# RWKV layer of a two-layer decoder trunk: causal masks, Gram products and the first T products tied to other matmuls

## The chip, the core and the metric

The kernel runs on one core of one Trainium2 chip. The core has five engines that run their own instruction queues in order and wait for each other through semaphores: TensorE (PE, with its weight loads as PEld), VectorE (DVE), ScalarE (ACT), GpSimd (POOL) and SyncE (SP), beside 16 DMA engines. The metric is the time on the device in microseconds (us) of one execution; lower is better. Three runs of the kernel before are there, and one more execution was taken by the hardware profiler.

## The reference

An input of 512 tokens by 2048 channels in float32 passes two residual layers, first a gated differential attention, then a gated RWKV-7 time mixing. The change lies in the second. Cut to what matters:

```python
def rwkv7_mixer(h, ...):
    p = h @ w_in                          # r, k, v, gate: 2048 columns each; decay and rate: 96 each
    p = p + (token_shift(p) - p) * mu
    r, k, v, g, dw, da = split(p)
    decay = exp(-exp(-softplus(-(w0 + tanh(dw) @ decay_up)) - 0.5))
    a = sigmoid(a0 + da @ iclr_up)
    kk = heads(k * k_k); kk = kk / norm(kk)
    k = k * (1 + (a - 1) * k_a)
    y = wkv7_scan(r, decay, k, v, -kk, kk * a)      # 32 heads of 64 channels
    y = group_norm(y) + sum(r * k * r_k) * v
    return (y * silu(g)) @ w_out

def step(S, r, w, k, v, a, b):            # one token of one head, S is 64 x 64
    sa = S @ a
    S = S * w + outer(sa, b) + outer(v, k)
    return S, S @ r
```

## The kernel before

**Tiling.** The second layer works on 16 pairs of heads, `j` = 0 to 15, of 128 channels each. For each pair there are four projections (`k`, `r`, `v` and, three pairs late, the gate). One is 48 matmuls of 128x128 weights by 512 tokens on TensorE: 16 slices of the 2048 inputs, each as three products of high and low parts (`mm3`, L129). The weights come in raw by DMA, are cast to `wh` on ScalarE (L115), and VectorE makes the rest `wl` (L116). "The 27th receptance matmul" is a place in such a run of 48: hooks in the list `behind` are called when their number of matmuls has been issued.

**The scan.** The 512 tokens are cut into 8 chunks of 64, and a chunk's recurrence is made of matrix products. For a pair this takes, in order: `stage1` and `stage2` build `AR` (the scaled kk and r; L1122 finishes it with the receptances) and `BK`; `gram` multiplies `BK` by `AR` for all chunks (`gp`, L1137), and ScalarE copies the parts into `LP` (L1145) and the whole into `G` (L1150). `mask_gram` clears what is not causal in `G`, with four `affine_select` on POOL, two of 64x512 (L1182) and two of 64x1024 elements (L1184). `t_solve` inverts a triangular 32x32 matrix for each chunk and half on VectorE: it transposes `LP` to `LT` (L1216), scales by `n` (the norms of the keys, which come over a DMA issued on POOL), then makes 31 steps of a product (L1230) and a sum (L1233) on `Tm`, then transposes to `T` (L1238, the tile `T1`) and to `W` (L1243); POOL copies `W` into `TT` (four copies, L1249) and fills a new `Tm` from `unit` (L1220). `t_first` and `t_second` are two groups of small products on TensorE (`px`, L1264 from `T`, and L1279 from `W`) with ScalarE copies, which complete `TT`.

Then `scan_pair` goes through the 8 chunks. Each has three products on TensorE one after the other: `sm` from `VS` and `G` (L1356), from `rhs` and `TT` (L1369), from `VS` and `BKT` (L1378). Between them ScalarE copies (L1359, L1371), and the state is renewed by VectorE (`VS`, L1385 for the first chunk, L1382 later), which needs `Sg` from POOL (L1364 copies `SA`, L1367). At the end stand the outputs `Y` (L1402, L1406) and their normalisation on VectorE and ScalarE (L1417 to L1433).

**What sets the order.** The program is written for a list scheduler, which puts each engine's instructions in one fixed order. All pairs are staggered: while the projections of pair `j` run, the scan of pair `j-1` is woven in as a generator whose steps come every few matmuls (`Chain`, `tick`), and the solve of pair `j` is another generator (`Solve`): a `yield n` in `t_solve` lets n matmuls pass. A hook's work is placed behind its matmul by `issue_after` (on TensorE) or by `behind` (masks and solve), which gives the scheduler an order without a semaphore; when the chip runs it, the engine's own queue and true data dependences decide. `LAG` is 3; the hooks are 12, 15 or 18 in the value projection for `gram`, and in the receptance projection of the next pair 6 for the masks, 12 and 33 for the two `px` groups and 39 or 45 for the norms.

Of the kernel before, what the change touches and what calls it, by code (L numbers as in the profile page):

```python
# [942 lines left out]
@urgent  # L943
def shift_mix(g, ps, rows, mu, omu, tag, bufs=2):

    nc, w = g.nc, g.work
    o_ = w.tile([P, T], F32, name="mix" + tag, tag=tag, bufs=bufs)
    nc.scalar.activation(o_[:rows, :], ps[:rows, :], AF.Copy, scale=omu)
    nc.vector.scalar_tensor_tensor(o_[:rows, 1:], ps[:rows, 0 : T - 1], mu, o_[:rows, 1:], ALU.mult, ALU.add)
    return o_  # L950
# [77 lines left out]
LAG = 3  # L1028
# [6 lines left out]
def mus(g, i, j):  # L1035
    n = i * 16 + j
    return g.mu[:, n : n + 1], g.omu[:, n : n + 1]
# [121 lines left out]
def norms(g, j, p, m):  # L1159

    nc, w = g.nc, g.work
    while g.later:
        g.later.pop(0)()
    ps = g.ps.tile([P, 512], F32, name="pt", tag="pb", bufs=2)
    with g.tc.issue_after(m.ins):
        sum_channels(g, ps[:2, :], g.ones[:, 0 : P : C], p.k2)
    ss = w.tile([2, T], F32, name="ssl", tag="thg", bufs=1)
    nc.scalar.copy(ss[:].rearrange("h (b c t) -> h c b t", b=2, c=NC_), ps[:2, :].rearrange("h (c b t) -> h c b t", c=NC_, b=2))
    nd = g.nd[j % 2]
    for half in range(2):  # L1170
        x = ss[:, half * NC_ * HALF : (half + 1) * NC_ * HALF]
        nc.gpsimd.dma_start(out=nd[:, half].rearrange("h r c t -> h r (c t)"),
                            in_=x[:, None].to_broadcast([2, NG, NC_ * HALF]))
    p.n2 = g.small.tile([P, HALF], F32, name="n2", tag="n2", bufs=1)
    nc.gpsimd.dma_start(out=p.n2[:], in_=nd.rearrange("h b r c t -> (h b r c) t"))


def mask_gram(g, p, h, m=None):

    nc = g.nc  # L1180
    for r_ in [slice(h * C, h * C + C)]:
        a = nc.gpsimd.affine_select(out=p.G[r_, :, 0, 1 - h, :], in_=p.G[r_, :, 0, 1 - h, :], compare_op=ALU.is_ge,  # L1182
                                fill=0.0, base=-1, pattern=[[0, NC_], [1, C]], channel_multiplier=-1)
        b = nc.gpsimd.affine_select(out=p.G[r_, :, 1], in_=p.G[r_, :, 1], compare_op=ALU.is_ge, fill=0.0, base=0,  # L1184
                                pattern=[[0, NC_], [0, 2], [1, C]], channel_multiplier=-1)
        behind(g, a, m)
        behind(g, b, m)


def turn_keys(g, p, c0):  # L1190

    nc = g.nc
    if not c0:
        p.BKT = g.work.tile([P, NC_, P], F32, name="BKT", tag="BKT", bufs=2)
    ps = g.ps.tile([P, 512], F32, name="pt", tag="pb", bufs=2)
    for i in range(4):
        nc.tensor.transpose(ps[:, i * P : (i + 1) * P], p.BK[:, c0 + i].rearrange("p s t -> p (s t)"), g.ident[:])
    nc.scalar.copy(p.BKT[:, c0 : c0 + 4], ps[:].rearrange("p (c k) -> p c k", c=4))


def behind(g, ins, m=None):

    m = m or g.at
    if m:
        g.tc.add_manual_dep(ins.ins, m.ins.name, mybir.DependencyInfo(mybir.DependencyClass.NoSync,
                            mybir.DependencyReason.DATA), reason="pace")


def t_solve(g, j, p):


    nc, w = g.nc, g.work
    NQ = HALF // NG
    yield 6
    LT = w.tile([P, HALF, HALF], F32, name="LT", tag="LT", bufs=1)
    lt = nc.vector.transpose(LT[:].rearrange("p (r c) t -> p t r c", r=NG),  # L1216
                        p.LP[:].rearrange("p c t -> p t c")[:, :, None, :].to_broadcast([P, HALF, NG, NC_]))
    Tm = w.tile([P, NQ, HALF], F32, name="Tm", tag="Tm", bufs=1)
    tmp = w.tile([P, NQ * HALF], F32, name="tmpl", tag="tmpl", bufs=1)
    nc.gpsimd.tensor_copy(Tm[:], g.unit[:])  # L1220
    n2 = p.n2
    behind(g, lt)
    with g.tc.issue_after(lt.ins):
        nc.vector.tensor_scalar(n2[:], n2[:], 1e-24, None, ALU.max)
        nc.vector.reciprocal(n2[:], n2[:])
    yield 9 if j >= LAG else 3
    for i in range(HALF - 1):
        n, s = HALF - 1 - i, i // NG + 1
        tt = tmp[:, : n * s].rearrange("p (a b) -> p a b", a=s)
        st = nc.vector.scalar_tensor_tensor(tt, LT[:, i : i + 1, i + 1 :].to_broadcast([P, s, n]), n2[:, i : i + 1],  # L1230
                                       Tm[:, 0:s, i : i + 1].to_broadcast([P, s, n]), ALU.mult, ALU.mult)
        behind(g, st)
        nc.vector.tensor_add(Tm[:, 0:s, i + 1 :], Tm[:, 0:s, i + 1 :], tt)  # L1233
        yield 3 + i % 2
    nc.vector.tensor_mul(Tm[:], Tm[:], n2[:, None, :].to_broadcast([P, NQ, HALF]))
    p.T1 = w.tile([P, NC_, HALF], F32, name="T1", tag="T1", bufs=1)
    yield 9
    tt = nc.vector.transpose(p.T1[:].rearrange("p c (q r) -> p q r c", r=NG),  # L1238
                        Tm[:].rearrange("p q (r c) -> p q r c", r=NG))
    p.W = w.tile([P, NC_, HALF], F32, name="W", tag="Tm", bufs=1)  # L1240
    behind(g, tt)
    yield 4
    tt = nc.vector.transpose(p.W[:], p.T1[:])  # L1243
    behind(g, tt)
    for h in range(2):
        for half in range(2):
            o = half * HALF
            q = slice(h * C + o, h * C + o + HALF)
            nc.gpsimd.tensor_copy(g.TT[j % 2][q, :, h, o : o + HALF], p.W[q])  # L1249
# [72 lines left out]
def gated(g, j, p, gt, last=False):  # L1322
    g.nc.vector.tensor_mul(gt[:], gt[:], p.y[:])
    if last:
        return
    g.nc.scalar.dma_start(out=g.yd2[j * P : (j + 1) * P, :], in_=gt[:])
# [118 lines left out]
def layer1(g, aps):  # L1445
    nc, tc = g.nc, g.tc
    with ExitStack() as cx:
# [5 lines left out]
        pairs = []  # L1453

        def proj(i, j, **k):
            return unit_chan(g, [(win, i * D + j * P, P)], P, **k)[0]
# [10 lines left out]
        def receptances(j):  # L1467
            def piece(f, i, p):
                def follow(m):
                    with tc.high_priority(offset=SCAN), tc.issue_after(m.ins):  # L1470
                        f(g, i, p)
                return follow

            behind = [(45 if j == 1 else 39, lambda m: norms(g, j, pairs[j], m))]
            if j:
                behind += [(6, lambda m: [mask_gram(g, pairs[j - 1], h, m) for h in range(2)]),
                           (12, piece(t_first, j - 1, pairs[j - 1])),
                           (33, piece(t_second, j - 1, pairs[j - 1]))]
            return shift_mix(g, proj(0, j, behind=behind), P, *mus(g, 0, j), "r", 1)

        begin(0)
        r = receptances(0)
        for j in range(D // P):
            p = pairs[j]
            if j:
                others = [(1, lambda p=p: turn_keys(g, p, 0)), (2, lambda p=p: turn_keys(g, p, 4)),
                          (4, lambda p=p: turn_values(g, p))]
                if j > 1:
                    others.append((5, lambda i=j - 2: finish_y(g, i, pairs[i])))
                full = LAG <= j < D // P - 1  # L1490
                gaps = (7, 8) if full else (5, 6) if j == 2 else (4, 5) if j == 1 else (6, 7)
                chain(g, j - 1, pairs[j - 1], 3 if j > 1 else 22, *gaps, others)
            stage2(g, j, r, p)

            def behind(m, j=j, p=p):
                if j > 1:
                    pairs[j - 2].chain.finish(g)
                with tc.issue_after(m.ins):
                    gram(g, j, p)
                p.solve = Solve(g, t_solve(g, j, p))  # L1500
            hooks = [(12 if 0 < j < LAG else 15 if j else 18, behind)]
            if j + 1 == D // P:
                hooks.append((39, lambda m, p=p: [mask_gram(g, p, h, m) for h in range(2)]))
            stage_v(g, j, p, proj(2, j, behind=hooks))
            turns = ()
            if j == 0:
                turns = ((9, lambda m: turn_keys(g, p, 0)), (15, lambda m: turn_keys(g, p, 4)),
                         (27, lambda m: turn_values(g, p)))
            if j + 1 < D // P:
                begin(j + 1, turns)  # L1510
            if j >= LAG:
                gated(g, j - LAG, pairs[j - LAG], gate(g, j - LAG, proj(3, j - LAG)))
            if j + 1 < D // P:
                r = receptances(j + 1)
# [121 lines left out]
```

## Time and profile before

| | us |
|---|---|
| median of three runs | 2165.76 |
| lowest and highest of them | 2164.96, 2167.0 |
| the profiled execution | 2167.01 |
| its span, first to last instruction | 2165.1 |
| second layer's pairs 4 to 14: one pair's period (`gp` to `gp`) | 60.9 |
| busy in the 60 us from 1480: PE, DVE, ACT, POOL | 58.82, 52.61, 37.05, 17.44 |

The granted TensorE clock is 0.999 of full speed. The second layer's pairs run from about 1014 to 1970 us of the span. Engines are named as in the section on the chip; L12 is line 12 of the kernel. In the timeline a row gives the start in us, the length in us, engine, line, operation and tiles, and in brackets the idle time of its engine before it and what ended that. Rows that follow each other are pipelined, so their lengths overlap a little; a step's cost is read from start to start. Profiled matmul ends are modelled.

### The profile page before, as it was taken

How to read it: one execution, taken by the hardware profiler on the slowest of the kernel's cores; microseconds unless marked ns; L12 is line 12 of the kernel's file. 1: busy time of each engine (PE TensorE's matmuls, PEld its weight loads, DVE VectorE, ACT ScalarE, POOL GpSimd, SP SyncE). 2: the span in 40 equal slices, each digit the busy share in tenths (PEclk: the TensorE clock that was granted, in tenths of full speed). 3: DMA queues.
4: the chain of work that ended last, by engine and by line, in shares of the span. 5: the costliest groups of instructions: out<-in, count | busy, mean ns of one | idle time of the engine just before them, and what ended most of it. 6: DMA issues, size and time to landing. Idle time of an engine off the chain costs nothing.

```text
span 2165.1 us, 34929 instructions
## 1 busy us (share of the span) xinstructions
PE 2129.7 (98%) x12260; PEld 1752.7 (81%) x12260; DVE 1557.4 (72%) x4137; ACT 1126.3 (52%) x2587; POOL 337.4 (16%) x614
## 2 busy tenths in 40 slices
PE   9999999999999999999999999999999999999999
PEld 7888888888888877888777888878887888877887
DVE  5665647465656667467889888888888888887645
ACT  6443444343444455345566665666666665665333
POOL 0000000000000000011132332233333332232001
PEclk9999999999999999999999999999999999999999
DMA  6223232322223365662322222232222223345565
GB/s 196 90 88 98 79 102 85 96 94 87 92 88 98 98 204 177 189 138 84 88 60 67 76 67 79 77 85 76 76 76 77 76 67 79 82 129 173 188 169 120
DMA packets 258623, 225.76 MB, mean 104 GB/s; under 512 B 12336, under 2 KB 220480, under 8 KB 258448
## 3 DMA queue, kind: packets, MB, share of 16 engines
q1 hardware_dynamic: 239504, 188.03, 29.4%
q0 software_dynamic: 10080, 19.50, 4.5%
q10 hardware_dynamic: 8864, 16.01, 2.0%
q8 instruction: 96, 1.57, 0.3%
q14 instruction: 79, 0.65, 0.1%
HBM read 207.50 MB, written 15.99 MB: 103 GB/s over the span
## 4 chain that ended last, share of the span: by engine, by line
PE 82%; DVE 11%; ACT 3%; issue 3%; DMA 1%; ACTq 0%; DVEq 0%
PE pp L129 63%; PE pt L129 5%; DVE wl L116 2%; PE gp L1137 1%; DVE tmpl L1230 1%; PE o L129 1%; PE sc L129 1%; PE sm L1356 1%; PE lora L129 1%; DVE Tm L1233 1%; PE sm L1378 1%; ACT wh L115 1%; DMA yr<-yd 1%; PE Y L1402 1%; PE sm L1369 1%
## 5 line engine op out<-in xcount | busy, mean ns | idle before, releaser
L116 DVE TENSOR_TENSOR wl<-wraw,wh 128x512 fp32r<-128x512 f32 (+1 forms) x636 | 449.6, 709 | 345.5 <-ACT wh L115 336.6
L115 ACT CAST wh<-wraw 128x512 fp32r<-128x512 f32 (+1 forms) x636 | 392.8, 619 | 499.6 <-PE pp L129 391.9
L129 PE MATMUL pp<-wh,hH 128*128 128x512 f32 x1268 | 500.2, 394 | 0.7 <-DVE prmin_rw_mu_dram L234 0.6
L129 PE MATMUL pp<-wh,hL 128*128 128x512 f32 x1268 | 497.5, 393 | 0.1
L129 PE MATMUL pp<-wl,hH 128*128 128x512 f32 x1268 | 497.2, 392 | 0.0
L129 PE MATMUL pp<-hH,wh 128*128 128x512 f32 x1024 | 417.5, 408 | 0.0
L129 PE MATMUL pp<-hL,wh 128*128 128x512 f32 x1024 | 413.2, 404 | 0.0
L129 PE MATMUL pp<-hH,wl 128*128 128x512 f32 x1024 | 412.7, 403 | 0.0
L129 PEld LDWEIGHTS pp<-wh,hH 128*128 128x128 f32 x1268 | 238.3, 188 | 49.9 <-issue 1.7
L129 PEld LDWEIGHTS pp<-wh,hL 128*128 128x128 f32 x1268 | 238.2, 188 | 49.2 <-DVE hL L908 0.5
L129 PEld LDWEIGHTS pp<-wl,hH 128*128 128x128 f32 x1268 | 238.3, 188 | 46.9
L129 PEld LDWEIGHTS pp<-hH,wh 128*128 128x128 f32 x1024 | 193.0, 189 | 37.3 <-issue 1.8
L129 PEld LDWEIGHTS pp<-hH,wl 128*128 128x128 f32 x1024 | 193.2, 189 | 33.4
L129 PEld LDWEIGHTS pp<-hL,wh 128*128 128x128 f32 x1024 | 193.2, 189 | 32.0
L1230 DVE SCALAR_TENSOR_TENSOR tmpl<-LT,n,Tm 128x60 f32<-128x60 f32 (+24 forms) x496 | 148.4, 299 | 12.1
L1364 POOL COPY SA<-VS 64x64 f32<-64x64 f32 x224 | 72.4, 323 | 513.2 <-DVE VS L1382 441.6
L500 POOL DMA_DIRECT2D frow<-yd x12 | 8.9, 742 | 801.8 <-DVE rs_t L67 675.9
L1233 DVE TENSOR_TENSOR Tm<-Tm,tmpl 128x60 f32<-128x60 f32 (+24 forms) x496 | 114.5, 231 | 13.1
L1359 ACT COPY rhs<-sm 64x64 f32<-64x64 f32 x256 | 52.6, 205 | 63.2 <-PE sm L1356 60.4
L1371 ACT COPY VS<-sm 64x64 f32<-64x64 f32 x256 | 52.8, 206 | 58.2 <-PE sm L1369 51.7
L1382 DVE SCALAR_TENSOR_TENSOR VS<-sm,gam,Sg 64x64 f32<-64x64 f32 x192 | 54.0, 281 | 30.6 <-PE sm L1378 26.3
L1356 PEld LDWEIGHTS sm<-VS,G 128*128 128x128 f32 x256 | 46.5, 188 | 26.1 <-PE pp L129 13.1
(339 smaller groups left out, 3268.0 us busy)
## 6 DMA issues: line engine op xcount, KB each, us to landing
wraw<-in_rw_w_in_dram SPq DMA_DIRECT2D x128, 512.0 KB, 4.0
wraw<-in_da_w_in_dram SPq DMA_DIRECT2D x254, 256.0 KB, 3.0
wraw<-in_da_w_out_dram SPq DMA_DIRECT2D x26, 512.0 KB, 4.3
wraw<-in_rw_w_out_dram SPq DMA_DIRECT2D x26, 512.0 KB, 4.3
yr<-yd SPq DMA_DIRECT2D x28, 256.0 KB, 3.9
frow<-yd POOLq DMA_DIRECT2D x12, 512.0 KB, 7.1
xq<-in_x_dram SPq DMA_DIRECT2D x16, 256.0 KB, 5.4
xd<-xq ACTq DMA_DIRECT2D x16, 256.0 KB, 4.1
```

Of the source, the lines that this page charges most:

```text
L115: nc.scalar.copy(hi[:], raw[:, k : k + n])
L116: nc.vector.tensor_sub(lo[:], raw[:, k : k + n], hi[:].bitcast(F32))
L129: m = nc.tensor.matmul(out, a, b, start=s, stop=e, skip_group_check=skip)
L1137: m = nc.tensor.matmul(gp[h][:, i * P : (i + 1) * P], BK[r_, c0 + i, :, :], p.AR[r_, c0 + i, :, :], start=True, stop=True)
L1230: st = nc.vector.scalar_tensor_tensor(tt, LT[:, i : i + 1, i + 1 :].to_broadcast([P, s, n]), n2[:, i : i + 1], Tm[:, 0:s, i : i + 1].to_br ...
L1233: nc.vector.tensor_add(Tm[:, 0:s, i + 1 :], Tm[:, 0:s, i + 1 :], tt)
L1356: nc.tensor.matmul(sm[:, 0:P], both(p.G[:, c, 0]), both(VS[:, c]), start=True, stop=True)
L1359: rc = nc.scalar.copy(rhs[r_, :], sm[r_, h * C : h * C + C])
L1364: nc.gpsimd.tensor_copy(p.SA[r_, c - 1, :], VS[r_, c, h, :])
L1369: nc.tensor.matmul(sm[:, P : P + C], both(g.TT[j % 2][:, c]), rhs[:], start=True, stop=True)
L1371: vc = nc.scalar.copy(VS[r_, c, h, :], sm[r_, P : P + C])
L1382: g.state = nc.vector.scalar_tensor_tensor(VS[r_, c + 1, h, :], s_, p.gam[r_, c : c + 1], Sg[r_, :], ALU.mult, ALU.add)
```

## The change

The masks of pair `j-1` are tied to the 27th receptance matmul in place of the 6th. The Gram products of pairs 3 to 15 come behind the 18th value matmul in place of the 15th. The solve's first pause is 3 matmuls in place of 6, and its second 10 or 6 in place of 9 or 3, so that counted from the value projection's start the transposition stands where it stood in pairs 3 to 15, and the first step one matmul later. For pair 0 alone the two `px` groups are tied to the 18th and 39th matmul in place of the 12th and 33rd.

```diff
 def t_solve(g, j, p):
-    yield 6
+    yield 3
     LT = w.tile([P, HALF, HALF], F32, name="LT", tag="LT", bufs=1)
...
-    yield 9 if j >= LAG else 3
+    yield 10 if j >= LAG else 6
     for i in range(HALF - 1):
...
             if j:
-                behind += [(6, lambda m: [mask_gram(g, pairs[j - 1], h, m) for h in range(2)]),
-                           (12, piece(t_first, j - 1, pairs[j - 1])),
-                           (33, piece(t_second, j - 1, pairs[j - 1]))]
+                behind += [(27, lambda m: [mask_gram(g, pairs[j - 1], h, m) for h in range(2)]),
+                           (12 if j > 1 else 18, piece(t_first, j - 1, pairs[j - 1])),
+                           (33 if j > 1 else 39, piece(t_second, j - 1, pairs[j - 1]))]
...
-            hooks = [(12 if 0 < j < LAG else 15 if j else 18, behind)]
+            hooks = [(12 if 0 < j < LAG else 18, behind)]
```

On POOL, at the end of a scan and the start of the next (the same in all pairs from 3 on; `SA` and `Sg` belong to the scan that ends, `TT`, `G` and `Tm` to the next pairs), there stood before:

```order
L1367 TENSOR_SCALAR Sg<-SA,gam 128x64
L1182 AFFINE_SELECT G_12753<-G_12753 64x8x64
L1184 AFFINE_SELECT G_12753<-G_12753 64x8x128
L1364 COPY SA<-VS 64x64
L1182 AFFINE_SELECT G_12753<-G_12753 64x8x64
L1364 COPY SA<-VS 64x64
L1249 COPY TT_10024<-W 32x8x32 x4
L1184 AFFINE_SELECT G_12753<-G_12753 64x8x128
L1353 MEMSET VS 64x64 x2
L1220 CAST Tm<-unit 128x256
```

and now there stands:

```order
L1367 TENSOR_SCALAR Sg<-SA,gam 128x64
L1364 COPY SA<-VS 64x64 x2
L1249 COPY TT_10024<-W 32x8x32 x4
L1182 AFFINE_SELECT G_12759<-G_12759 64x8x64
L1184 AFFINE_SELECT G_12759<-G_12759 64x8x128
L1182 AFFINE_SELECT G_12759<-G_12759 64x8x64
L1353 MEMSET VS 64x64 x2
L1184 AFFINE_SELECT G_12759<-G_12759 64x8x128
L1220 CAST Tm<-unit 128x256
```

All four masks moved behind the copies from `W`, and so behind the end of the solve. In pair 1 they moved behind the last `SA` copies and the `MEMSET`, ahead of the TT copies; in pair 2 behind the last `SA` copies; pair 0's and the last pair's did not move.

On VectorE, at the end of a solve (`T` is the tile that the first `px` products read, the last row here the state that the scan's last chunk needs), before:

```order
L1233 TENSOR_TENSOR Tm<-Tm,tmpl 128x8
L1235 TENSOR_TENSOR Tm<-Tm,n_12700 128x256
L1238 STREAM_TRANSPOSE T_13203<-Tm 128x32x8
L116 TENSOR_TENSOR wl<-wraw,wh 128x512
L949 SCALAR_TENSOR_TENSOR mixv<-pp,prmin_rw_mu_dram,mixv 128x511
L1382 SCALAR_TENSOR_TENSOR VS<-sm,gam,Sg 64x64 x2
```

and now:

```order
L1233 TENSOR_TENSOR Tm<-Tm,tmpl 128x8
L1235 TENSOR_TENSOR Tm<-Tm,n_12700 128x256
L116 TENSOR_TENSOR wl<-wraw,wh 128x512
L1238 STREAM_TRANSPOSE T_13204<-Tm 128x32x8
L949 SCALAR_TENSOR_TENSOR mixv<-pp,prmin_rw_mu_dram,mixv 128x511
L1382 SCALAR_TENSOR_TENSOR VS<-sm,gam,Sg 64x64 x2
```

`T` and a weight split changed places. Earlier in the solve some splits and mixes moved past one or two solve steps in the same way; between `W` and `AR` nothing moved on VectorE.

On TensorE, in the value projection of each pair from 3 to 14 (a piece of the difference):

```order
 L129 MATMUL pp<-hL,wh 128x512
 L129 MATMUL pp<-hH,wl 128x512
+L129 MATMUL pp<-hH,wh 128x512
+L129 MATMUL pp<-hL,wh 128x512
+L1378 MATMUL sm<-VS,BKT 128x128
+L129 MATMUL pp<-hH,wl 128x512
 L1137 MATMUL gp<-AR,BK 128x128 x16
-L129 MATMUL pp<-hH,wh 128x512
-L129 MATMUL pp<-hL,wh 128x512
-L1378 MATMUL sm<-VS,BKT 128x128
-L129 MATMUL pp<-hH,wl 128x512
```

Three projection matmuls and one of the scan's products now stand ahead of the Gram products; in the last pair three projection matmuls. Nothing else moved on TensorE, the `px` groups of pair 0 included, and the number of its instructions is the same.

## The prediction

> **What bounds the kernel now.** I read the page's first part, then TensorE's waits for the stretch from 1187 to 1918 us, in which twelve pairs run alike, then the timelines of one of these pairs. The first fence is the page's line of busy times and the waits of that stretch (who waits, for whom: us in total, times, longest).
>
> ```profile
> PE 2129.7 (98%) x12260; PEld 1752.7 (81%) x12260; DVE 1557.4 (72%) x4137; ACT 1126.3 (52%) x2587; POOL 337.4 (16%) x614
> PE sm L1356 <- DVE VS L1382: 6.6, 12, 0.6
> PE gp L1137 <- DVE AR L1122: 5.0, 11, 0.5
> PE px L1264 <- DVE T L1238: 2.0, 12, 0.2
> ```
>
> TensorE is the bound, and no matmul is added or taken away. What an order can win in that stretch is its idle time, 6.6 + 5.0 + 2.0 = 13.6 us, some 1.17 us a pair, all three waits being for VectorE. Here is one pair where `px` and the scan's last product wait (timeline rows: start, us, engine, line; in brackets the idle time before).
>
> ```profile
> 1526.66 0.19 DVE L1233 TENSOR_TENSOR Tm<-Tm,tmpl 128x28 f32<-128x28 f32 x1
> 1528.90 0.23 DVE L1230 SCALAR_TENSOR_TENSOR tmpl<-LT,n,Tm 128x24 f32<-128x24 f32 x1
> 1529.05 1.21 POOL L1182 TENSOR_SCALAR_AFFINE_SELECT G<-G 64x512 f32<-64x512 f32 x1
> 1529.65 0.64 DVE L1233 TENSOR_TENSOR Tm<-Tm,tmpl 128x24 f32<-128x24 f32 x1
> 1530.23 1.69 POOL L1184 TENSOR_SCALAR_AFFINE_SELECT G<-G 64x1024 f32<-64x1024 f32 x1
> 1530.82 1.12 DVE L1230 SCALAR_TENSOR_TENSOR tmpl<-LT,n,Tm 128x16 f32<-128x16 f32 x1
> 1534.14 0.64 DVE L1238 STREAM_TRANSPOSE T<-Tm 128x256 f32<-128x256 f32 x1
> 1534.63 0.67 DVE L116 TENSOR_TENSOR wl<-wraw,wh 128x512 fp32r<-128x512 f32 x1
> 1534.93 0.69 PE L1264 MATMUL px<-T,G 32*32 32x32 f32 x32 [0.18 <-DVE T L1238]
> 1535.22 0.73 DVE L949 SCALAR_TENSOR_TENSOR mixv<-pp,prmin_rw_mu_dram,mixv 128x511 f32<-128x511 f32 x1
> 1535.87 0.58 DVE L1382 SCALAR_TENSOR_TENSOR VS<-sm,gam,Sg 64x64 f32<-64x64 f32 x2
> 1536.60 0.46 PE L1356 MATMUL sm<-VS,G 128*128 128x128 f32 x2 [0.55 <-DVE VS L1382]
> ```
>
> The reader is to see two solve steps that take 0.64 and 1.12 us beside a mask on POOL, where equal or larger ones take 0.19 and 0.23 without. That is 0.45 + 0.89 = 1.3 us lost by VectorE just ahead of the two results TensorE waits for.
>
> **The change part by part.** *Masks behind the TT copies.* By the order, the two masks that stood ahead of the last `SA` copies now stand behind the TT copies, so the 1.3 us above are free. `T` goes behind a weight split (L116) in VectorE's order, which puts it 0.6 us back (1534.63 to 1535.22). `T` ends at 1534.78 now, so at 1534.78 - 1.3 + 0.6 = 1534.1; `px` could start at 1534.93 - 0.18 = 1534.75, with 0.6 us in hand. `VS` ends at 1536.45, so at 1535.15; the `sm` behind it was free at 1536.60 - 0.55 - 0.18 = 1535.87, with 0.7 in hand. Bounds: if nothing is lifted, `T` ends at 1535.4, `px` waits 0.75 and `sm` not at all, 0.75 for 0.73 now, no gain; if all of it is, 6.6 + 2.0 = 8.6 us. Since some 0.75 of the 1.3 suffices, I take **-8.6**.
>
> *Gram products three matmuls later.* The second place is the chain to `AR`, which the masks now fall into.
>
> ```profile
> 1536.49 0.66 POOL L1182 TENSOR_SCALAR_AFFINE_SELECT G<-G 64x512 f32<-64x512 f32 x1
> 1541.25 1.16 POOL L1184 TENSOR_SCALAR_AFFINE_SELECT G<-G 64x1024 f32<-64x1024 f32 x1
> 1541.31 1.64 DVE L116 TENSOR_TENSOR wl<-wraw,wh 128x512 fp32r<-128x512 f32 x1 [0.57 <-ACT wh L115]
> 1543.91 0.76 DVE L1417 TENSOR_REDUCE s<-Y 128x4 f32<-128x256 f32 x2
> 1548.66 1.16 POOL L1172 DMA_DIRECT2D nd<-ssl  x2 [3.65 <-ACT ssl L1168]
> 1549.11 0.38 PE L1356 MATMUL sm<-VS,G 128*128 128x128 f32 x2
> 1552.20 0.69 DVE L1122 TENSOR_TENSOR AR<-mixr,E 128x512 f32<-128x512 f32 x1
> 1552.95 2.06 PE L1137 MATMUL gp<-AR,BK 64*128 64x128 f32 x32 [0.45 <-DVE AR L1122]
> 1494.39 0.40 PE L129 MATMUL pp<-hL,wh 128*128 128x512 f32 x1
> 1495.08 0.39 PE L129 MATMUL pp<-hH,wh 128*128 128x512 f32 x1
> ```
>
> Of the four instructions that `gp` now follows, three (a `pp`, `sm`, a `pp`) take 1495.08 - 1494.39 = 0.69 in the pair before, the fourth another 0.23: 0.92. TensorE without waits reaches `gp` at 1552.50 - 0.73 + 0.92 = 1552.69; `AR` ends at 1552.89. So `AR` must come 0.2 earlier, and else `gp` waits. Two effects oppose. VectorE, which has no other change of order between `VS` and `AR`, enters this stretch up to 1.3 us earlier. And POOL runs four masks in it in place of two, of which only the L1184 above costs much now: 1.64 - 0.69 = 0.95. What four in a row cost is seen in pair 1, where they run beside the solve:
>
> ```profile
> 1114.60 0.60 DVE L1230 SCALAR_TENSOR_TENSOR tmpl<-LT,n,Tm 128x54 f32<-128x54 f32 x1
> 1115.23 1.08 DVE L1233 TENSOR_TENSOR Tm<-Tm,tmpl 128x54 f32<-128x54 f32 x1
> 1116.36 0.66 DVE L1230 SCALAR_TENSOR_TENSOR tmpl<-LT,n,Tm 128x48 f32<-128x48 f32 x1
> 1117.05 1.09 DVE L1233 TENSOR_TENSOR Tm<-Tm,tmpl 128x48 f32<-128x48 f32 x1
> 1166.16 1.01 POOL L1182 TENSOR_SCALAR_AFFINE_SELECT G<-G 64x512 f32<-64x512 f32 x1
> 1166.58 0.74 DVE L949 SCALAR_TENSOR_TENSOR mixk<-pp,prmin_rw_mu_dram,mixk 128x511 f32<-128x511 f32 x1
> 1120.56 0.46 PE L1356 MATMUL sm<-VS,G 128*128 128x128 f32 x2 [1.01 <-DVE VS L1382]
> 1127.36 0.69 PE L1264 MATMUL px<-T,G 32*32 32x32 f32 x32 [0.62 <-DVE T L1238]
> ```
>
> 3.43 us for four steps that take 2 x (0.23 + 0.19) = 0.84 alone: 2.6 lost. In the `AR` stretch part is covered. The split at 1541.31 waits 0.57 for its cast anyway, which takes in the first L1182's 0.45. The two reductions (0.76) read PSUM, and an instruction that does (L949 at 1166.58, 0.74 beside a mask, 0.73 without) loses nothing. That leaves 2.6 - 0.45 - 0.76 = 1.4, or 0.45 more than now, and `AR` 1.3 - 0.45 = 0.85 earlier; as what TensorE feeds moves up by 0.73 only, 0.4 to 0.7 is likelier. The new wait s lies between 0 and, with nothing covered (2.6 - 0.95 - 1.3 = 0.35 later: 1553.24 + 0.05 - 1552.69), 0.6. The margin is thin, so I take s = 0.1: **-5.0 + 11 x 0.1 = -3.9**.
>
> Behind the masks on POOL stand the `Tm` cast and the norms' DMA: POOL idles 3.65 us before that DMA at 1548.66. The masked `G` is first read at 1549.11, while four masks (3.6 us) behind TT copies end near 1545. If that cover were gone, the next scan's first product would wait.
>
> *The solve starts later against TensorE*: `gp` moves up 0.26 (1552.95 to 1552.69), all behind it 0.73 + 0.45 = 1.18, so `LT`, which needs the products copied, loses 0.9. VectorE's idle times take that in:
>
> ```profile
> 1501.05 0.69 DVE L116 TENSOR_TENSOR wl<-wraw,wh 128x512 fp32r<-128x512 f32 x1 [0.76 <-ACT wh L115]
> 1513.71 0.60 DVE L1382 SCALAR_TENSOR_TENSOR VS<-sm,gam,Sg 64x64 f32<-64x64 f32 x2 [0.60 <-PE sm L1378]
> 1921.19 2.21 DVE L1216 STREAM_TRANSPOSE LT<-LP 128x1024 f32<-128x1024 f32 x1 [1.01 <-ACT LP L1145]
> ```
>
> 0.76 + 0.60 against 0.9, so 0 (bare, it would be up to 0.9 a pair). In the last pair nothing is won ahead of `gp`, and `LT` (1921.19) already waits for the products: three matmuls of 0.23 later, between 0 and 0.7; I take **+0.65**.
>
> *First pairs.* Pair 1's masks go behind the scan's end, so 2.6 us leave the way to the waits of 1.01 and 0.62; they then meet the tail of the solve and the next `AR`. Between 0 and 1.6; I take **-1.0**. Pair 2's masks only pass two copies and still run before `T`: 0. Pair 0's later hooks (18 and 39) move nothing on TensorE by the order: 0.
>
> Sum: -8.6 - 3.9 + 0.65 - 1.0 = -12.85. Span 2165.1 becomes 2152.25; with the 1.9 around it (2167.0 profiled) 2154.1; the median of the runs, 2165.76, lies 1.25 below the profiled one: **2153 us**.
>
> **The rivals.** *A, AR stays late.* The masks are not covered, s is 0.35 to 0.6: 2.75 to 5.5 us dearer, 2156 to 2158.5, up to 2160 if pair 1 gains nothing. For it: the margin of 0.2. Against: the 0.57 idle.
>
> *B, slower.* The four masks cost VectorE their full length in the `AR` stretch, 2 x (0.66 + 1.16) = 3.6, and the head start is only TensorE's 0.73, because the split waits for its cast: `AR` 3.6 - 0.95 - 0.73 = 1.9 later, s = 1552.89 + 1.9 + 0.05 - 1552.69 = 2.15. That is -8.6 - 5.0 + 11 x 2.15 + 0.65 = +10.7: 2176. It turns the sign from s = 13.6 / 11 = 1.24. Against it: 2.6, not 3.6, in pair 1. The Trainium skill states such a rule: in "SBUF — State Buffer", section "Who interferes with whom", a VectorE instruction with two SBUF inputs and a GpSimd one that reads SBUF exclude each other, the later one blocked for the whole of the earlier. By that rule it is 2176; the trace agrees in kind and shows less in size, 0.89 lost to a mask of 1.16.
>
> *C, no change.* The long solve steps don't come from the masks, or others take their place: `px` waits 0.75 twelve times, `gp` no longer: -13.6 + 9.0 + 0.65 = -3.95, 2161.8. Against it: four steps in pair 1 show the same.
>
> *D, the masks' tie does nothing*, as it orders without a wait. POOL's order differs, so I give it no chance of its own; only for pair 0's hooks it holds.
>
> **How the numbers follow.** Forecast 57%, with its own range 2150 to 2156; A 22%; C 11%; B 8%; something else 2%. The lowest is all 13.6 and 1.6 gained: 2150.6, less 1 for the runs' scatter. So 2149 to 2162, which holds A and half of C. About 0.2%, 4.3 us, can be told from no change: faster 80%, within 11%, slower 9%.
>
> **What would show it.** In the changed profile: no L1230 or L1233 above 0.5 us near the end of a solve; no `px` and `sm` waits between pairs 3 and 15; a `gp` wait under 0.2; long VectorE instructions behind `W` in place of them. A `gp` wait above 1.24 us, or `px` waits of 0.75, would make the prediction wrong.

## The result, and the profile after

The changed kernel takes 2154.3 us (median of four runs, 2152.45 to 2155.93). Four runs of the kernel before, taken beside it, have a median of 2166.04. The ratio is 0.9946, with an interval from 0.9928 to 0.9963: faster by about half a per cent. The profiled execution has a span of 2152.0 us, where the prediction said 2152.25 and 2153 for the time. The total came out nearly as forecast, but two of its terms did not, and their errors have opposite signs.

Where the 13.2 us of span came from is read at the first Gram matmul of each pair (`gp`, L1137), whose start stands in the timeline. The change puts `gp` of pairs 3 to 15 some 0.92 us later in TensorE's own order, which is taken out in the last column.

| stretch | before, us | after, us | difference | without the later place of `gp` | forecast |
|---|---|---|---|---|---|
| start to `gp` of pair 0 | 1041.60 | 1040.21 | -1.4 | -1.4 | 0 |
| `gp` of pair 0 to that of pair 3 | 146.13 | 152.57 | +6.4 | **+5.5** | -1.0 |
| `gp` of pair 3 to that of pair 15 | 730.09 | 711.85 | -18.2 | **-18.2** | -12.5 |
| `gp` of pair 15 to the end | 247.31 | 247.32 | 0.0 | +0.9 | +0.65 |

The first line holds nothing that the change touches, and stands for how much two executions differ. The next fence has TensorE's waits in the changed kernel, in two answers of one view: the first two rows from the first pairs (1000 to 1187 us; the smaller ones are left out), the last three from all that comes later (1187 to 1990). The columns are who waits, for whom: us in total, times, longest.

```profile
PE px L1264 <- DVE T L1238: 7.0, 3, 3.1
PE sm L1356 <- DVE VS L1385: 1.4, 1, 1.4
...
PE sm L1356 <- DVE VS L1382: 0.9, 1, 0.9
PE sm L1369 <- ACT rhs L1359: 0.6, 1, 0.6
PE sm L1378 <- ACT VS L1371: 0.3, 1, 0.3
```

The last three rows are the whole of the later stretch, each of them once, in the last pair. The three waits of the kernel before, 6.6 for `VS`, 5.0 for `AR` and 2.0 us for `T`, have no row in pairs 3 to 14 any more. In the first pairs it is the other way: `px` waits 7.0 us in three pairs where it waited 2.8.

Here is the piece of the timeline that answers to the one shown of before: the end of the solve in the same pair of the changed kernel (start, us, engine, line).

```profile
1525.28 0.23 DVE L1230 SCALAR_TENSOR_TENSOR tmpl<-LT,n,Tm 128x24 f32<-128x24 f32 x1
1526.03 0.18 DVE L1233 TENSOR_TENSOR Tm<-Tm,tmpl 128x24 f32<-128x24 f32 x1
1526.73 0.23 DVE L1230 SCALAR_TENSOR_TENSOR tmpl<-LT,n,Tm 128x16 f32<-128x16 f32 x1
1529.64 0.65 DVE L1238 STREAM_TRANSPOSE T<-Tm 128x256 f32<-128x256 f32 x1
1530.72 0.58 DVE L1382 SCALAR_TENSOR_TENSOR VS<-sm,gam,Sg 64x64 f32<-64x64 f32 x2
1531.07 0.69 PE L1264 MATMUL px<-T,G 32*32 32x32 f32 x32
```

The two steps that took 0.64 and 1.12 us take 0.18 and 0.23. `T` ends at 1530.29, 0.8 us ahead of the `px` that reads it, and no row has a bracket. Next come the masks, now behind the copies from `W`, and VectorE on its way to `AR`:

```profile
1536.26 1.59 POOL L1184 TENSOR_SCALAR_AFFINE_SELECT G<-G 64x1024 f32<-64x1024 f32 x1
1536.76 1.64 DVE L917 TENSOR_TENSOR sLx<-k,sHx 128x512 fp32r<-128x512 f32 x1
1537.92 0.99 POOL L1182 TENSOR_SCALAR_AFFINE_SELECT G<-G 64x512 f32<-64x512 f32 x1
1538.32 0.86 DVE L917 TENSOR_TENSOR sLup<-upw,sHup 96x256 fp32r<-96x256 f32 x1
1539.21 0.76 DVE L1417 TENSOR_REDUCE s<-Y 128x4 f32<-128x256 f32 x2
1547.73 0.69 DVE L1122 TENSOR_TENSOR AR<-mixr,E 128x512 f32<-128x512 f32 x1
1548.70 0.49 PE L1137 MATMUL gp<-AR,BK 64*128 64x128 f32 x4
```

The long VectorE instructions have not gone; they have moved behind `W`, to `sLx` (1.64 us) and `sLup` (0.86). The two reductions of 0.76 are as long as before. `AR` still ends at 1548.42, 0.28 ahead of `gp`.

### The profile page after: what moved, and what is told of

Same layout as the page of the kernel before. It is cut to its first block, busy times and chain, and to the rows that moved or that the text cites. A ratio compares the mean times of both kernels' runs of the same rounds, so it can differ in the third digit from the quotient of the medians.

```text
span 2152.0 us, 34955 instructions
## 1 busy us (share of the span) xinstructions
PE 2128.2 (99%) x12260; PEld 1756.2 (82%) x12260; DVE 1547.9 (72%) x4137; ACT 1125.5 (52%) x2587; POOL 340.3 (16%) x614
## 4 chain that ended last, share of the span: by engine, by line
PE 92%; DVE 5%; ACT 1%; issue 1%; DMA 1%; POOL 0%; DVEq 0%; ACTq 0%; POOLq 0%
PE pp L129 72%; PE pt L129 5%; PE gp L1137 1%; PE o L129 1%; PE sm L1356 1%; PE sc L129 1%; PE sm L1378 1%; PE lora L129 1%; PE sm L1369 1%; PE Y L1402 1%; DMA yr<-yd 1%; DVE wl L116 1%; PE pt L1197 1%; PE pt L346 1%; PE z L129 1%
## 5 line engine op out<-in xcount | busy, mean ns | idle before, releaser
L116 DVE TENSOR_TENSOR wl<-wraw,wh 128x512 fp32r<-128x512 f32 (+1 forms) x636 | 439.2, 693 | 346.9 <-ACT wh L115 337.2
L1230 DVE SCALAR_TENSOR_TENSOR tmpl<-LT,n,Tm 128x60 f32<-128x60 f32 (+24 forms) x496 | 137.6, 277 | 13.1
L1233 DVE TENSOR_TENSOR Tm<-Tm,tmpl 128x60 f32<-128x60 f32 (+24 forms) x496 | 108.7, 219 | 13.8
L396 ACT ACTIVATE p<-sc,nb,sq 128x128 f32<-128x128 f32 (+3 forms) x64 | 39.0, 613 | 41.2 <-DVE nb L393 41.0
```

Source lines behind the costliest of these rows:

```text
L116: nc.vector.tensor_sub(lo[:], raw[:, k : k + n], hi[:].bitcast(F32))
L396: nc.scalar.activation(p_[:, :N], s[:, :N], AF.Exp, bias=nb[:, c : c + 1], scale=sq[:, t, c : c + 1], accum_out=sm[:, c : c + 1])
```

## The experiments

Nine kernels were run, in three batches. Times are medians; each batch had its own runs of the kernel before (2165.76, 2166.3 and 2166.35).

### One part alone

**The masks alone.** The kernel before with nothing but the masks' tie:

```diff
-                behind += [(6, lambda m: [mask_gram(g, pairs[j - 1], h, m) for h in range(2)]),
+                behind += [(27, lambda m: [mask_gram(g, pairs[j - 1], h, m) for h in range(2)]),
```

> Only the masks are tied to the 27th matmul; Gram products, pauses and the order of all engines but POOL as before. Theory: px and sm waits of pairs 3 to 14 gone as in the changed kernel, but TensorE comes to the Gram products 0.92 us earlier than there, where it has about 0.2 in hand, so these wait 0.7 in 11 pairs (0.45 before); pairs 1 and 2 lose as in the changed kernel; 2162 us. Rival (the gain is from the Gram products' place and what it does to VectorE's order): px and sm waits stay at 0.16 and 0.55, 2166 us or more.

Measured: 2163.05, ratio 0.9988 (0.9979 to 0.9997). TensorE's waits from 1187 to 1918 us are now one row:

```profile
PE gp L1137 <- DVE AR L1122: 8.9, 11, 0.8
```

The waits for `T` and `VS` are gone, and the wait for `AR` has grown from 0.45 to 0.8 us. In the two traces the instructions of TensorE, VectorE and ScalarE stand in the same order; only POOL's differs. This shows that those two came from the masks, and that TensorE, which arrives earlier, just waits at the next place.

**The Gram products alone.** The kernel before with the other edits, for pairs 3 to 15:

```diff
-    yield 6
+    yield 3 if j >= LAG else 6
...
-    yield 9 if j >= LAG else 3
+    yield 10 if j >= LAG else 3
...
-            hooks = [(12 if 0 < j < LAG else 15 if j else 18, behind)]
+            hooks = [(12 if 0 < j < LAG else 18, behind)]
```

> Gram products at the 18th matmul and the pauses of pairs 3 to 15; masks at the 6th; POOL's order as before. Theory: no gp waits, and px waits 0.75 in 12 pairs, as the masks still hold up the solve and T stands behind a weight split; 2159 us. Rival (masks do not matter): px waits under 0.3 and the whole gain of the later pairs, 2149 us.

Measured: 2158.76, ratio 0.9967 (0.9954 to 0.998). The one row of the same view:

```profile
PE px L1264 <- DVE T L1238: 7.4, 12, 0.6
```

`gp` waits no longer; `px` waits 0.6 us in place of 0.2. This is the regime that rival C described, and it is what is left when the masks stay on the solve.

**Half of the masks.** The kernel before, leaving out the two 64x1024 masks of pairs 3 to 14:

```diff
-def mask_gram(g, p, h, m=None):
+def mask_gram(g, p, h, m=None, wide=True):
...
-        b = nc.gpsimd.affine_select(out=p.G[r_, :, 1], in_=p.G[r_, :, 1], compare_op=ALU.is_ge, fill=0.0, base=0,
+        b = wide and nc.gpsimd.affine_select(out=p.G[r_, :, 1], in_=p.G[r_, :, 1], compare_op=ALU.is_ge, fill=0.0, base=0,
                                 pattern=[[0, NC_], [0, 2], [1, C]], channel_multiplier=-1)
...
-        behind(g, b, m)
+        _ = wide and behind(g, b, m)
...
-                behind += [(6, lambda m: [mask_gram(g, pairs[j - 1], h, m) for h in range(2)]),
+                behind += [(6, lambda m: [mask_gram(g, pairs[j - 1], h, m, j <= LAG) for h in range(2)]),
```

> The kernel before without the two 64x1024 masks of pairs 3 to 14, so the chunks' outputs of these pairs are not causal; no other engine's order differs. Theory (a mask holds up VectorE's instructions): the solve steps near 1530 fall to 0.65 and 0.23 us, so 0.9 of the 1.3 us are back, px and sm wait under 0.1, and AR comes 0.95 or more earlier, so gp does not wait; 2149 to 2152 us. Rival (the long steps have another cause): steps of about 1.1 us stay, waits as before, 2166 us.

Measured: 2155.18 in one run. The time fell by 10.6, less than expected, and the view says why:

```profile
PE sm L1356 <- DVE VS L1382: 3.5, 12, 0.3
```

The two 64x512 masks that are left now stand together beside the solve, and still cost it two steps:

```profile
1524.37 0.64 DVE L1233 TENSOR_TENSOR Tm<-Tm,tmpl 128x24 f32<-128x24 f32 x1
1525.54 0.62 DVE L1230 SCALAR_TENSOR_TENSOR tmpl<-LT,n,Tm 128x16 f32<-128x16 f32 x1
```

The changed kernel has 0.18 and 0.23 there. So both kinds of mask weigh on the solve.

The four kernels can be set side by side by a pair's period, the time from `gp` to `gp` between pairs 4 and 14, and by what the profile shows as waits in it:

| kernel | period, us | above 59.32 | waits that the profile shows |
|---|---|---|---|
| before | 60.86 | 1.54 | 0.55 + 0.45 + 0.17 = 1.17 |
| masks alone | 60.21 | 0.89 | 0.81 (`gp`) |
| Gram products alone | 60.16 | 0.84 | 0.62 (`px`) |
| half of the masks | 59.86 | 0.54 | 0.29 (`sm`) |
| the change | 59.32 | 0 | none |

Each part alone wins 0.65 or 0.70 of the 1.54, together they win all of it, 0.19 more than the sum. And every row costs more than its waits show; the section on the prediction comes back to that.

### The first pairs

**The change for pairs 3 to 15 alone**, the first pairs as before:

```diff
-    yield 3
+    yield 3 if j >= LAG else 6
...
-    yield 10 if j >= LAG else 6
+    yield 10 if j >= LAG else 3
...
-                behind += [(27, lambda m: [mask_gram(g, pairs[j - 1], h, m) for h in range(2)]),
+                behind += [(27 if j > LAG else 6, lambda m: [mask_gram(g, pairs[j - 1], h, m) for h in range(2)]),
```

> The change for pairs 3 to 15 alone; the masks of pairs 1 and 2 and the pauses of the solves of pairs 0 to 2 as before. Theory (POOL's masks block VectorE; in pairs 1 and 2 the change moved them onto the last solve steps): the px waits of pairs 1 and 2 fall from 3.09 and 2.62 us to the 0.6 and 0.9 of before, with waits of about 1.0 before the scan's product back; Gram products of pair 0 to those of pair 3 take 147 us in place of 152.6; the pairs behind keep their 59.3 us; 2149 us. Rival (the early pairs lose because TensorE comes earlier into them, or by scatter): 2154 us, px waits above 2 us.

Measured: 2148.49, ratio 0.9922 (0.9909 to 0.9934), which beats both kernels.

**The masks of the first pairs alone put back**: only the last of these three edits.

> The changed kernel with one thing put back: the Gram masks of the first three pairs (those followed up by pairs 1 to 3) are tied to the sixth receptance matmul again; the two pauses stay changed for every pair. Theory (in pairs 1 and 2 the masks tied to the 27th matmul land on the tail of the triangular solve, and that costs the first pairs about 5 us): from the first to the fourth Gram product of the pairs about 147.1 us as in the kernel before with the Gram at 18 (the changed kernel has 152.6), TensorE's waits for T in pairs 1 and 2 back to 0.6 and 0.9 us, and a median near 2149. Rival (the changed pauses of the first pairs, 3 and 6 in place of 6 and 3, delay the solve there): the stretch stays above 151 us and the median near 2154.

Measured: 2148.04, ratio 0.9917 (0.9901 to 0.9934); from `gp` of pair 0 to that of pair 3 it takes 147.36 us, where the change takes 152.57. It equals the run before within the spread of both, so the pauses of the first pairs are worth nothing. From the changed kernel it differs in POOL's order alone, so the whole loss there comes from the masks' place. Here are `px` of pair 1 and the matmuls behind it, without and with the late masks: first with the masks put back,

```profile
1125.95 0.69 PE L1264 MATMUL px<-T,G 32*32 32x32 f32 x32 [0.62 <-DVE T L1238]
1126.91 0.40 PE L129 MATMUL pp<-hL,wh 128*128 128x512 f32 x1
1127.14 0.39 PE L129 MATMUL pp<-hH,wl 128*128 128x512 f32 x1
```

and then the changed kernel, from the end of the scan's outputs (`Y`) on (three of the four masks, then VectorE, then TensorE):

```profile
1121.94 0.33 POOL L1353 MEMSET VS<- 64x64 f32 x2 [2.91 <-PE Y L1402]
1122.32 0.68 POOL L1182 TENSOR_SCALAR_AFFINE_SELECT G<-G 64x512 f32<-64x512 f32 x1
1122.96 1.69 POOL L1184 TENSOR_SCALAR_AFFINE_SELECT G<-G 64x1024 f32<-64x1024 f32 x1
1125.33 1.33 POOL L1184 TENSOR_SCALAR_AFFINE_SELECT G<-G 64x1024 f32<-64x1024 f32 x1
1122.33 0.69 DVE L1230 SCALAR_TENSOR_TENSOR tmpl<-LT,n,Tm 128x8 f32<-128x8 f32 x1
1123.54 1.13 DVE L1233 TENSOR_TENSOR Tm<-Tm,tmpl 128x8 f32<-128x8 f32 x1
1125.57 1.13 DVE L1418 TENSOR_SCALAR s<-s 128x4 f32<-128x4 f32 x1
1126.93 0.59 DVE L1238 STREAM_TRANSPOSE T<-Tm 128x256 f32<-128x256 f32 x1
1127.58 0.69 PE L1264 MATMUL px<-T,G 32*32 32x32 f32 x32 [3.09 <-DVE T L1238]
1129.03 0.63 PE L129 MATMUL pp<-hH,wl 128*128 128x512 f32 x1
1129.45 0.63 PE L129 MATMUL pp<-hH,wh 128*128 128x512 f32 x1
...
1181.28 0.69 PE L1264 MATMUL px<-T,G 32*32 32x32 f32 x32 [2.62 <-DVE T L1238]
```

The changed kernel's windows show the clock (the stretch, its length, busy us of PE, PEld, DVE, ACT and POOL, then TensorE's granted clock, DMA share, GB/s):

```profile
1128.50:1131.00 2.50, 2.50 (x10) 1.47 (x10) 1.86 (x6) 2.39 (x5) 2.36 (x4) 0.50 0.00 0
```

Two things are to be seen. The masks, which follow the `MEMSET` and so the end of the scan, meet the last steps of the solve, and three VectorE instructions between 1122 and 1127 take 0.69, 1.13 and 1.13 us where 0.22, 0.16 and 0.16 do without. And behind the wait of 3.09 us the matmuls start 0.42 us apart (1129.03, 1129.45) where they start 0.23 apart with the masks put back: TensorE's granted clock is 0.50.

### The masks' price, and the pauses

**The masks twice.** The changed kernel, the masks of pairs 3 to 14 issued twice, the second time without effect on `G`:

```diff
-                behind += [(27, lambda m: [mask_gram(g, pairs[j - 1], h, m) for h in range(2)]),
+                behind += [(27, lambda m: [mask_gram(g, pairs[j - 1], h, m) for _ in range(2 if j > LAG else 1) for h in range(2)]),
```

> The changed kernel with the masks of pairs 3 to 14 issued twice in a row (the second time they change nothing), so that GpSimd spends about 4.2 us more right behind them while VectorE works towards AR. Theory (VectorE cannot run its two-input instructions beside a mask, and AR has only about 0.2 us in hand): the wait of the Gram product for AR returns with 1 to 2.5 us in each of eleven pairs, and the time is 2166 to 2182. Rival (the masks cost nothing wherever they lie; the gain came from the Gram product's place alone): no wait of the Gram product, 2153 to 2156.

Measured: 2164.0 in one run, between the two. The wait for `AR` is back, with 8.1 us in eleven pairs, as the theory said, but with 0.74 each rather than 1 or more. In this kernel's timeline:

```profile
1547.38 0.66 POOL L1182 TENSOR_SCALAR_AFFINE_SELECT G<-G 64x512 f32<-64x512 f32 x1
1547.71 0.35 DVE L1430 TENSOR_SCALAR var<-var 128x8 f32<-128x8 f32 x1
1548.59 1.58 POOL L1184 TENSOR_SCALAR_AFFINE_SELECT G<-G 64x1024 f32<-64x1024 f32 x1
1549.06 1.12 DVE L67 TENSOR_TENSOR rs_t<-rs_i 128x8 f32<-128x8 f32 x1
1553.82 0.69 DVE L1122 TENSOR_TENSOR AR<-mixr,E 128x512 f32<-128x512 f32 x1
1554.57 0.60 PE L1137 MATMUL gp<-AR,BK 64*128 64x128 f32 x6 [0.74 <-DVE AR L1122]
```

Of the four added masks two delay VectorE, by 0.35 - 0.17 and 1.12 - 0.16, together 1.14 us; the other two run while it waits or reduces. From the last `VS` (1535.79) to the end of `AR` it takes 18.7 us here and 17.7 in the changed kernel; 1.02 longer less a wait of 0.74 leaves 0.28, which is what `AR` had in hand there.

**The second pause back at 9**, which puts `T` ahead of the weight split again:

```diff
-    yield 10 if j >= LAG else 6
+    yield 9 if j >= LAG else 6
```

> The changed kernel with the second pause of pairs 3 to 15 at 9 in place of 10, which puts the first T product ahead of the weight split again on VectorE; all else as in the change. Theory (the pauses are worth nothing once the masks are off the solve, since px does not wait): same as the changed kernel, 2154 within 1.5, and no wait for T in pairs 3 to 14. Rival (the later first steps of the solve are part of the gain): a wait for T of 0.2 us or more in each of twelve pairs and a median of 2157 or more.

Measured: 2154.32, ratio 0.9945 (0.993 to 0.996), no wait for `T` in pairs 3 to 14. It equals the change: the solve's later first step and the exchange of `T` with the split are worth nothing, with 0.8 us in hand.

### Covering the first pairs' wait

**Both `px` groups of pairs 1 and 2 later**, in the changed kernel:

```diff
-                           (12 if j > 1 else 18, piece(t_first, j - 1, pairs[j - 1])),
-                           (33 if j > 1 else 39, piece(t_second, j - 1, pairs[j - 1]))]
+                           (12 if j > LAG else 18, piece(t_first, j - 1, pairs[j - 1])),
+                           (33 if j > LAG else 39, piece(t_second, j - 1, pairs[j - 1]))]
```

> The changed kernel with the two px groups of pairs 1 and 2 tied to the 18th and 39th receptance matmul in place of the 12th and 33rd (as the change does for pair 0); some nine matmuls, 1.6 to 1.9 us, then run ahead of the wait for T. In the changed kernel TensorE idles 3.09 and 2.62 us there, and afterwards, for 3.4 us each time, its 128x512 matmuls start 0.43 us apart in place of 0.23 at a granted clock of 0.50. Theory (the idle time itself makes the clock fall): the waits shrink to 0.7 to 1.5 us, no stretch of pairs 1 and 2 shows a granted clock under 0.9, and the time falls by the shorter waits, 3.5, and by the slow matmuls, 2.6, to 2147 to 2149.5. Rival (the clock falls for another reason, so that only the waits shrink): matmuls 0.43 us apart stay behind px, and the time is 2150.5 to 2152.

Measured: 2155.34, ratio 0.9947 (0.9932 to 0.9962): no gain. Both the theory and its rival missed, since the waits did not shrink as both assumed: they are 2.81 and 2.72 us where they were 3.09 and 2.62 (pair 1, TensorE and VectorE):

```profile
1125.67 0.40 PE L129 MATMUL pp<-hH,wh 128*128 128x512 f32 x1
1127.62 0.68 DVE L1095 TENSOR_TENSOR l<-mixk,l 128x512 f32<-128x512 f32 x1
1128.23 0.60 DVE L1238 STREAM_TRANSPOSE T<-Tm 128x256 f32<-128x256 f32 x1
1128.88 0.69 PE L1264 MATMUL px<-T,G 32*32 32x32 f32 x32 [2.81 <-DVE T L1238]
1130.78 0.63 PE L129 MATMUL pp<-hH,wl 128*128 128x512 f32 x1
```

TensorE does run more matmuls ahead of `px`, up to 1125.67 in place of 1124.10. But `t_first` begins by finishing the solve (`p.solve.finish`), so a later hook puts the rest of the solve behind other work in VectorE's queue too: `AR` (L1094) and `l` (L1095) now run ahead of `T`, which comes at 1128.23 in place of 1126.93. VectorE has no idle time in the 8 us ahead of that `T`: the wait is not TensorE being early, VectorE is the bound there. Behind pair 2's wait, of 2.72 us, the clock stays at 0.50 for at least 7.8 us, as this kernel's windows show:

```profile
1183.20:1191.00 7.80, 7.80 (x49) 5.92 (x49) 4.86 (x14) 5.50 (x13) 3.94 (x6) 0.50 0.27 69
```

**The same, with the masks put back as well**: both edits together.

> As the run before, and the masks of the first three pairs back at the sixth receptance matmul: both ways of easing the first pairs together. Theory (the two waits for T that are left with the early masks, 0.6 and 0.9 us, are covered by the nine matmuls): those waits go, 2146 to 2147.5, the lowest of all. Rival (the later px only delays what TT needs, so the wait comes back at the second px group or at the next scan's product of rhs and TT): 2148 to 2149, no better than with the early masks alone.

Measured: 2148.43, ratio 0.9915 (0.9898 to 0.9931), no better than the masks put back alone. So far its rival was right, but in the main not for the rival's reason: `px` still waits 0.56 and 1.08 us for `T`, against 0.62 and 0.91 with the masks put back alone, and the wait that the rival named, at the second `px` group, is only 0.22.

The lowest are the three kernels with the first pairs' masks at the sixth matmul, 2148.0 to 2148.5. Of them the change with the one hook put back is the simplest.

## Why the prediction came out, and where its terms did not

**The bound and the mechanism held.** TensorE is the bound, and the gain of pairs 3 to 14 is its idle time. The masks on the solve caused the waits for `T` and `VS` (masks alone: both gone), the Gram products' place decided the wait for `AR` (Gram products alone: gone), and each part alone wins less than half of what both do. Rival C's case, `px` waiting 0.75, appears with 0.62 where the masks stay; rival D falls with the kernel that has only the tie. Rival A did not come: s is 0, as `AR` had about 0.3 us in hand (by the timeline and by the doubled masks) where the prediction had 0.2 and took 0.1 as a precaution.

**The masks in the `AR` stretch** cost VectorE 1.64 - 0.69 at `sLx` and 0.86 - 0.41 at `sLup`, 1.4 in all as in the prediction, and 0.4 at the first L1418 (0.55 in place of 0.16), of which the second gives back 0.2 (0.16 in place of 0.33). From the last `VS` to the end of `AR` it takes 17.7 us (1530.72 to 1548.42) where it took 17.0 (1535.87 to 1552.89): 0.7 longer, where the forecast was 0.45. The head start of VectorE, no longer held up in the solve, pays for it. Rival B, the full length of the four masks, is far off even with the masks doubled, where the added 3.6 us of masks cost 1.14. The rule of the Trainium skill that it drew on ("SBUF — State Buffer", section "Who interferes with whom") holds for the instructions that have two SBUF inputs: at L67 0.96 was lost to a mask of 1.58. Where the prediction read the trace as weaker than the rule (0.89 lost to a mask of 1.16), the step ends at 1530.82 + 1.12 = 1531.94 and the mask beside it at 1530.23 + 1.69 = 1531.92: what it lost is what was left of the mask. What the rule does not give is how many of a mask's microseconds meet such an instruction; here less than a third did.

**The size of the regular pairs' gain failed**, at the sentence "What an order can win in that stretch is its idle time, 6.6 + 5.0 + 2.0 = 13.6 us". It won 18.2. A wait costs TensorE more than the bracket shows. The first fence has the kernel before (with the rows at 1534.93 and 1536.60 that stand in the prediction),

```profile
1534.36 0.40 PE L129 MATMUL pp<-hH,wl 128*128 128x512 f32 x1
1535.55 0.49 PE L129 MATMUL pp<-hH,wh 128*128 128x512 f32 x1
1536.81 0.48 PE L129 MATMUL pp<-hL,wh 128*128 128x512 f32 x1
```

the second the same places in the changed kernel (with `px` at 1531.07):

```profile
1530.75 0.40 PE L129 MATMUL pp<-hH,wl 128*128 128x512 f32 x1
1531.70 0.50 PE L129 MATMUL pp<-hH,wh 128*128 128x512 f32 x1
1532.03 0.38 PE L1356 MATMUL sm<-VS,G 128*128 128x128 f32 x2
1532.17 0.48 PE L129 MATMUL pp<-hL,wh 128*128 128x512 f32 x1
```

From the matmul ahead to `px` it takes 0.57 with the wait and 0.32 without: 0.25, where the bracket says 0.18. To `sm` it is 1.05 and 0.33: 0.72, where it says 0.55; and the next matmul follows `sm` after 0.21 in place of 0.14. The bracket counts from the modelled end of the matmul ahead (0.40 or 0.49 long), but a matmul that need not wait starts before that end. For the three waits of a pair the period gives 1.54 against a shown 1.17; one wait alone hides between 0.08 (`gp`) and 0.25 (the shorter `sm`). The price of a wait is therefore read from start to start, against the same place without it.

**The first pairs failed**, at "Pair 1's masks go behind the scan's end, so 2.6 us leave the way to the waits of 1.01 and 0.62 [...] Between 0 and 1.6". The text named that the masks "then meet the tail of the solve" and gave it no price; for pair 2 it took 0. From pair 3 on the solve and the scan end together, and the masks fall behind the copies from `W`, past the solve. In pair 1 the last `VS` ends at 1118.1 us and `T` at 1127.5: the same tie puts the masks between them, on the solve's last steps, with nothing in hand. Pair 2 is alike: the last `VS` ends at 1171.5, the masks run from 1172.5 to 1178.6, four solve steps beside them take 0.58, 1.12, 0.62 and 1.12 us, and `T` ends at 1181.2.

The 5.2 us from `gp` to `gp` against the same kernel with the masks put back are made up as follows, from the starts of the same matmuls in both. At the two `px` that wait for `T` 2.5 and 1.8 are lost; at the two `sm` that waited 1.01 and 1.15, 1.2 and 1.3 are won; the last chunk of pair 2's scan loses some 0.6. The other 2.9 are slow matmuls behind the two waits, 1.4 to 1.5 each, at a granted clock of 0.50. The prediction's sum has no term for these, and they are more than half of the loss. With the masks alone, where the clock fell in pair 2 only, the stretch takes 150.07: 1.6 less than the changed kernel's 152.57 without the 0.92 of `gp`'s later place, which agrees with one fall less.

**The last pair** lost 0.9 where +0.65 was forecast: `LT` is late by the whole 0.92 of TensorE's order. Pair 0's hooks and the pauses are worth nothing, as forecast: with the first pairs as before but for these hooks, it takes 41.78 us from `gp` of pair 0 to that of pair 1, where the kernel before takes 41.76. The first pause of pairs 3 to 15 was not run apart.

So -12.85 came near to -13.2 by luck: two errors nearly cancel, 5.7 too little gain in the regular pairs and 6.5 too little loss in the first. And 1.4 of the 13.2 stand ahead of the first pair, where the two executions differ by chance; the rest, 11.8, is what the medians give (2166.04 to 2154.3).

## What to carry to other kernels

Where a wait is moved by taking something off one stretch, test at once what stands behind it: here each of the two edits alone won less than half, since TensorE reached the next late result sooner. A rule that is right in the steady state ("masks behind the last copies") should be read again at the first iterations, where other work ends last; one condition on the pair's number is worth 6 us here. And the worth of a wait is read from start to start, not from the bracket.

## What the runs showed of the hardware

**TensorE's clock fell to half after waits of 2.6 to 3.1 us in the middle of busy work, and elsewhere after shorter ones.** In the second layer's pairs, matmuls of 128x512 start 0.42 us apart in stretches of five of the eleven profiles, at a granted clock of 0.50: the change, the masks alone, the second pause at 9, the masks twice, and the later `px` groups. These are the five with waits of 2.59 to 3.09 us for `T`; in the six others the longest wait of TensorE in the pairs is 1.45 to 1.50, and there is no such stretch. Whether and when the clock falls varies: with the masks alone pair 1's wait of 3.08 is followed by none, while pair 2's of 2.60 is; in the changed kernel it falls 0.9 us after work resumed in pair 1, and 1.7 after in pair 2. The five also share the late masks of the first pairs. But the clock falls at some 980 us too, ahead of the pairs and of every mask in `G`, in eight of the eleven profiles. Here is the kernel before, behind waits of 0.57 and 1.70 us with 1.2 us of matmuls between them:

```profile
983.00:986.00 3.00, 3.00 (x15) 2.54 (x14) 2.76 (x14) 1.34 (x4) 0.00 (x0) 0.50 0.34 120
```

So the clock can fall without a late mask. Three profiles have much the same two waits there (0.58 to 0.88 and 1.71 to 1.73) and no fall, so the length of a wait alone does not decide, and what does was not shown. These stretches at 0.50 last 3.4, 6.8 or 10.2 us. The doubled masks of pairs 3 to 14, with waits of 0.74, leave the clock alone. The Trainium skill ("TensorE: Matmul & The Clock Gate", section "Part 1: The HAM clock gate") says that the clock is halved after an idle window of about 3.4 us, and that the window runs freely, so that the point varies. The traces agree in the half clock and in the scatter; waits shorter than that window, 2.6 us in the pairs, were enough here.

**A mask on GpSimd delays more than the two-input instructions.** Beside the 64x1024 mask the small `tensor_scalar` L1418 (128x4) took 1.13 us in place of 0.16, and L1430 (128x8) 0.35 in place of 0.17 beside a 64x512 one, while the reductions from PSUM (L1417, two in 0.76) took what they take alone.
